# State space output projection: the last two value chunks, with their gate chunks, by seven products instead of eight

## The chip, the cores and the metric

The kernel runs on one core of one Trainium2 chip. The metric is the device time of one execution, in microseconds, as the median of the runs. A separate profiled execution gives the page and the trace.

## The reference

The program is a decoder trunk of two layers on 256 tokens of width 2048. Each layer has a token mixer, an attention to 256 memory tokens and a squared-ReLU MLP, each with an RMS norm before it and a residual add after it; a last norm closes the trunk. The token mixer of layer 0 is a chunked gMLP, that of layer 1 a state space layer with a gated output:

```python
_, states = lax.associative_scan(combine, (a, bu), axis=0)
y = jnp.einsum('gcp,sbgp->bsgc', cmat, states).real + d_skip.astype(F32) * u
y = jax.nn.gelu(y.reshape(bsz, seq, B_WIDTH), approximate=False).astype(h.dtype)
val, gate = jnp.split(y @ w_out + b_out, 2, axis=-1)
return val * jax.nn.sigmoid(gate)
```

All of it is float32. The change touches only the last two lines: `y` is 256 x 2048, `w_out` 2048 x 4096, its left half giving the values and its right half the gates.

## The kernel before

**Precision.** A float32 operand is split into a high half (rounded to the fast matmul format, by ScalarE, L103) and a low half (the rest, by VectorE, L104). A product of two operands takes three matmuls: high by high, low by high, high by low.

**Tiling.** Contraction runs over 16 k tiles of 128. Weights come in raw tiles of two k tiles by 512 columns (512 KB), loaded on the SP queue by `wload` (L127) into four raw buffers, split by `wtile` into three buffers each for high and low halves (`whi`, `wlo`). For one such slice `gemm_tok` (L159) runs 12 matmuls of 128 x 512: two k tiles, two token tiles t, three products. The activations are the stationary operand. After each slice `tick` advances a plan of small delayed tasks (`at(delay, task)`).

**The stage.** `s5` runs the scan, chunk by chunk, and then the output projection. The output has four value chunks of 512 columns (0 to 3) and four gate chunks (numbered 4 to 7 in the weights, `NCH + j`). For each j the kernel computes value chunk j and gate chunk `NCH + j`, adds the biases from PSUM (L1443, L1444; each bias is a row broadcast to 128 partitions by a load on POOL's queue, L113), takes the sigmoid of the gate on ScalarE (L1445), multiplies (L1446) and adds to the residual x (L1447), all of them 1024 wide. One tick later the next norm takes the chunk: squares summed on ScalarE (L198), 8 transposes on TensorE (L236), scaling into high and low halves on ScalarE and VectorE (L245, L246). Chunks 0 and 1 are interleaved by k, because the last features of the scan come late; chunks 2 and 3 are four plain calls of `gemm_tok`.

**Seven products.** `gemm_seven` multiplies a block of 2 token tiles x 2 column chunks x 2 slices (four k tiles) by 7 products in place of 8, as in Strassen's scheme in Winograd's form, and the other slices of both chunks directly. It needs four combinations of the activations (`sums`, from `token_sums`), four raw weight tiles at once, a buffer `run` for combined weights (L821, L827, L834, L841 on VectorE), and four 512-wide homes in which ScalarE keeps partial results copied from PSUM (`keep`, L812). Its matmuls are at L776. Between the products it places direct slices, and it ends with two direct slices taken in halves, so that each pair of PSUM banks is closed on its own. Before the change it serves the attention's values and output projection, and the second MLP's down projection (there with blocks of eight k tiles). It takes two adjacent column chunks, `n0` and `n0 + 1`.

**Order.** A framework schedules each engine's instructions ahead of time, by program order among those ready in its own estimate of time, and adds the semaphores. Each engine then runs its list in that order. Buffers of a pool with the same tag share slots, and a new tile waits for the old one's last reader.

**Buffers named by the change.** In `s5`, `resp` is four tiles of 128 x 1024 with the response matrices of the scan (`dq` in the profile); tags `qq`, `us`, `vv`, `u` and `pq` belong to scan tiles of 128 x 1024 each. The scan has finished with them when chunk 1 of the output begins.

Of the kernel before, what the change touches and what calls it, by code (L numbers as in the profile page):

```python
# [9 lines left out]
F32 = mybir.dt.float32  # L10
F32R = mybir.dt.float32r
I32 = mybir.dt.int32
AF = mybir.ActivationFunctionType
ALU = mybir.AluOpType
AX = mybir.AxisListType

P = 128
D = 2048
S = 256
KT = D // P  # L20
NB = 512
NCH = D // NB
KB = 2
# [15 lines left out]
class Trunk:  # L39
# [707 lines left out]
                    made.add(k)  # L747
        return raw, t1, t2, load, add

    def gemm_seven(self, tiles, token, sums, w, n0, k0, gather, end=None, own=None, ahead=None, then=None):  # L750

        nc = self.nc
        v = nc.vector
        kc0 = k0 // KB
        ws, run, kept = tiles
        raw, half = {}, lambda t: t.rearrange("p (k c) -> p k c", k=KB)  # L760

        def fetch(i, j):
            t = ws()
            self.fed = nc.sync.dma_start(out=half(t), in_=w[n0 + j, kc0 + i]).ins
            raw[i, j] = t

        def parts(src, own=None):
            hi, lo = (own() if own else self.wp.tile([P, KB * NB], F32R, name=nm) for nm in ("whi", "wlo"))
            self.split(hi, lo, src)
            return half(hi), half(lo)  # L770

        begun = set()

        def into(key, kts, left, hi, lo):
            out = banks[key]
            mm = lambda s, m, e: nc.tensor.matmul(out, s, m, start=key not in begun, stop=e, skip_group_check=True)  # L776
            for kk in kts:
                ah, al = left(kk)
                mm(ah, hi[:, kk, :], False)
                begun.add(key)  # L780
                mm(al, hi[:, kk, :], False)
            for kk in kts:
                mm(left(kk)[0], lo[:, kk, :], True)

        def block(key, t, i, src, more=None):
            into(key, range(KB), lambda kk: token(KB * i + kk, t), *parts(src))
            if ahead:
                into(key, range(KB), lambda kk: token(KB * (2 + i) + kk, t), *parts(more))

        def summed(key, k, src, more=None):  # L790
            into(key, range(KB), lambda kk: [f[:, k, kk, :] for f in sums[0]], *parts(src, own))
            if ahead:
                into(key, range(KB), lambda kk: [f[:, k, kk, :] for f in sums[1]], *parts(more))

        todo = {j: list(range(4 if ahead else 2, KT // KB)) for j in range(2)}

        def direct(j, first):

            kc = todo[j].pop(0)
            hi, lo = self.wtile(w, n0 + j, kc0 + kc)  # L800
            for t in (first, 1 - first):
                into((t, j), range(KB), lambda kk: token(KB * kc + kk, t), hi, lo)
                yield
            self.tick()

        def whole(*a):
            for _ in direct(*a):
                pass

        def keep(key, i):  # L810
            t = kept(i)
            nc.scalar.copy(out=t, in_=banks[key])  # L812
            return t

        acc = [self.psA.tile([P, 2, NB], F32, name="acc") for _ in range(2)]
        banks = {(1, 0): acc[0][:, 0], (0, 1): acc[0][:, 1], (0, 0): acc[1][:, 0], (1, 1): acc[1][:, 1]}
        for i, j in ((0, 0), (0, 1), (1, 0), (1, 1)):
            fetch(i, j)
        run = run()
        far, t1, t2 = ahead[:3] if ahead else ({}, None, None)  # L820
        v.tensor_tensor(out=run, in0=raw[0, 1], in1=raw[0, 0], op=ALU.subtract)  # L821
        summed((0, 1), 0, run, t1)
        block((1, 0), 0, 0, raw[0, 0], far.get((0, 0)))
        m5, m1 = keep((0, 1), 0), keep((1, 0), 1)
        block((0, 0), 0, 1, raw[1, 0], far.get((1, 0)))
        whole(1, 1)
        v.tensor_tensor(out=run, in0=raw[1, 1], in1=run, op=ALU.subtract)  # L827
        if ahead:
            ahead[-1](1)
        summed((1, 0), 1, run, t2)  # L830
        gather(0, n0, m1)
        u2 = keep((1, 0), 2)
        whole(1, 1)
        v.tensor_tensor(out=raw[0, 1], in0=raw[1, 1], in1=raw[0, 1], op=ALU.subtract)  # L834
        if ahead:
            ahead[-1](2)
        summed((1, 0), 2, raw[0, 1], far.get((0, 1)))
        gather(0, n0 + 1, u2)
        u3 = keep((1, 0), 3)
        whole(0, 0)  # L840
        v.tensor_tensor(out=run, in0=raw[1, 0], in1=run, op=ALU.subtract)  # L841
        if ahead:
            v.tensor_tensor(out=t1, in0=far[1, 0], in1=t2, op=ALU.subtract)
        block((1, 0), 1, 1, run, t1)
        whole(1, 1)
        summed((0, 1), 3, raw[1, 1], far.get((1, 1)))
        if then:
            then[-2]()
        v.tensor_tensor(out=u3, in0=u3, in1=m5, op=ALU.add)
        whole(0, 0)  # L850
        gather(1, n0 + 1, u3)
        while len(todo[0]) > 1 or len(todo[1]) > 1:
            j = len(todo[1]) > len(todo[0])
            whole(j, j)
        if then:
            then[-1](0)
        ends = [direct(0, 1), direct(1, 0)]
        for keys in (((1, 0), (0, 1)), ((0, 0), (1, 1))):
            for e in ends:
                next(e)  # L860
            for t, j in keys:
                (end or gather)(t, n0 + j, banks[t, j])
        for e in ends:
            next(e, None)
# [359 lines left out]
    def s5(self, x, cur, nxt):  # L1224
        nc, a, tc = self.nc, self.a, self.tc
        hT = cur.act
        NQ = G // NCH
        with tc.tile_pool(name="s5", bufs=2, reuse_waits="tile") as sp:
            yT = self.new_act()
            st = {}  # L1230

            ahead = {}
# [8 lines left out]
            resp = [sp.tile([P, T * P], F32, name=f"dq{i}", bufs=1) for i in range(4)]  # L1241
# [162 lines left out]
            for n in range(NCH):  # L1404
# [3 lines left out]
                chunks(n, acc)  # L1408
                follow(n)

            nxt.start()
            wo = a["b_w_out"]
            for j in range(NCH):
                if j == 0:
                    spare = self.psM.pop()
                    av1 = [spare.tile([P, NB], F32, name="ps") for _ in range(2)]
                    part = lambda n, acc, k: self.gemm_tok(yT, wo, n, acc=acc, kts=range(*k), first=k[0] == 0,
                                                           last=k[1] == KT)
                    av, _, ag = (part(n, acc, (0, 4)) for n, acc in ((0, None), (1, av1), (NCH, None)))
                    for k in (4, 8):  # L1420
                        for n, acc in ((0, av), (1, av1), (NCH, ag)):
                            part(n, acc, (k, k + 4))
                    self.flush()
                    for n, acc in ((0, av), (NCH, ag)):
                        part(n, acc, (12, KT))
                elif j == 1:
                    av = part(1, av1, (12, KT))
                    ag = self.gemm_tok(yT, wo, NCH + 1)
                else:
                    av = self.gemm_tok(yT, wo, j)  # L1430
                    ag = self.gemm_tok(yT, wo, NCH + j)
                cs = slice(j * NB, (j + 1) * NB)
                bv = self.bc(sp, a["b_b_out"][j * NB:(j + 1) * NB])
                bg = self.bc(sp, a["b_b_out"][D + j * NB:D + (j + 1) * NB])
                val = sp.tile([P, 2, NB], F32, name="val", tag="pq", bufs=4)
                gat = sp.tile([P, 2, NB], F32, name="gat", tag="pq", bufs=4)
                b2 = lambda b: b.unsqueeze(1).broadcast_to([P, 2, NB])
                if j == 1:
                    for t in range(2):
                        nc.vector.tensor_tensor(out=val[:, t], in0=av1[t], in1=bv, op=ALU.add)  # L1440
                    self.psM.append(spare)
                else:
                    nc.vector.tensor_tensor(out=val, in0=av, in1=b2(bv), op=ALU.add)  # L1443
                nc.vector.tensor_tensor(out=gat, in0=ag, in1=b2(bg), op=ALU.add)  # L1444
                nc.scalar.activation(out=gat, in_=gat, func=AF.Sigmoid)  # L1445
                nc.vector.tensor_tensor(out=val, in0=val, in1=gat, op=ALU.mult)  # L1446
                nc.vector.tensor_tensor(out=x[:, :, cs], in0=x[:, :, cs], in1=val, op=ALU.add)  # L1447
                self.at(1, lambda j=j: nxt.chunk(x, j))
# [185 lines left out]
```

## Time and profile before

| what | value |
|---|---|
| median of 3 runs | 2772.53 us (2771.16 to 2774.17) |
| profiled execution | 2768.95 us |
| its span, first to last instruction | 2767.2 us |
| granted TensorE clock in it | 0.999 |
| TensorE matmuls | 14978, busy 2747.1 us |
| VectorE | busy 2046.0 us |
| ScalarE | busy 1421.1 us |
| weights of the stage (`b_w_out`) | 64 loads of 512 KB, issued from 1474.6 to 1673.3 us |

The span is what the trace covers; the profiled execution's own time is 1.75 us longer, and differs from the median of the other runs by 3.6 us. In the rows, times are microseconds from the span's start unless marked ns; PE is TensorE's matmuls and PEld its weight loads, DVE is VectorE, ACT ScalarE, POOL GpSimd and SP the queue that issues most loads. A row of the timeline gives the start, the length, the engine, the line, what is written from what, and in brackets the idle time before it with what ended it. Overlapping matmuls make each row longer than the step from one to the next.

### The profile page before, as it was taken

The numbers are of one execution on the slowest core, as the hardware profiler recorded it, in microseconds if no ns is written. First come the engines' busy times: TensorE is split into PE (matmuls) and PEld (weight loads), VectorE is DVE, ScalarE is ACT, GpSimd is POOL, SyncE is SP. The second block draws the span as 40 slices with busy tenths as digits, with TensorE's granted clock in tenths as the row PEclk, the third lists the DMA queues.
The fourth block names the chain that finished last, engine by engine and source line by source line (L and its number), as shares of the span: only waits on it lengthen the run. The fifth ranks groups of instructions, "written<-read, shape, count | busy, mean of one in ns | idle before, by whom it ended". The sixth has DMA issues, their size and how long they took to land. (4 is left out here: it accounts for less than half of the span.)

```text
span 2767.2 us, 39486 instructions
## 1 busy us (share of the span) xinstructions
PE 2747.1 (99%) x14978; PEld 2326.5 (84%) x14978; DVE 2046.0 (74%) x2809; ACT 1421.1 (51%) x1814; POOL 186.7 (7%) x331
## 2 busy tenths in 40 slices
PE   9999999999999999999999999999999999999998
PEld 7888888888888888888888888888888888888887
DVE  6865756778888878787577667557767978869685
ACT  6545544555544434444566445445555655546454
POOL 0100000001011111111203100000000000000000
PEclk9999999999999999999999999999999999999999
DMA  8766665557788888886879767565557557475565
GB/s 298 231 196 230 202 183 181 170 159 231 220 281 258 262 258 256 266 256 221 235 238 288 214 202 231 182 195 153 182 163 232 176 174 244 153 248 163 177 212 159
DMA packets 194175, 593.75 MB, mean 215 GB/s; under 512 B 44096, under 2 KB 45168, under 8 KB 193472
## 3 DMA queue, kind: packets, MB, share of 16 engines
q1 hardware_dynamic: 153456, 537.46, 61.3%
q0 software_dynamic: 40000, 52.71, 6.8%
q8 instruction: 117, 1.92, 0.3%
q10 hardware_dynamic: 528, 1.06, 0.1%
q14 instruction: 74, 0.61, 0.1%
HBM read 567.51 MB, written 23.46 MB: 214 GB/s over the span
## 5 line engine op out<-in xcount | busy, mean ns | idle before, releaser
L104 DVE TENSOR_TENSOR wlo<-wraw,whi 128x1024 fp32r<-128x1024 f32 (+1 forms) x865 | 1051.3, 1221 | 444.5 <-ACT whi L103 438.2
L103 ACT CAST whi<-wraw 128x1024 fp32r<-128x1024 f32 (+1 forms) x865 | 909.2, 1053 | 812.2 <-PE acc L875 181.2
L174 PE MATMUL acc<-act,whi 128*128 128x512 f32 x3072 | 740.9, 391 | 0.6 <-DVE act L246 0.6
L174 PEld LDWEIGHTS acc<-act,whi 128*128 128x128 f32 x3072 | 563.1, 188 | 110.7 <-issue 1.4
L179 PEld LDWEIGHTS acc<-act,wlo 128*128 128x128 f32 x3072 | 395.0, 191 | 17.0 <-DVE wlo L104 1.4
L179 PE MATMUL acc<-act,wlo 128*128 128x256 f32 x3072 | 403.2, 283 | 1.2 <-DVE wlo L104 0.8
L159 PE MATMUL acc<-whi,act 128*128 128x512 f32 x1472 | 369.4, 393 | 5.4 <-ACT whi L103 5.4
L159 PEld LDWEIGHTS acc<-whi,act 128*128 128x128 f32 x1472 | 274.8, 189 | 62.6 <-ACT whi L103 5.6
L776 PE MATMUL acc<-whi,act 128*128 128x512 f32 x864 | 233.0, 392 | 0.1
L875 PE MATMUL acc<-whi,hl 128*128 128x512 f32 x544 | 212.7, 391 | 0.0
L874 PE MATMUL acc<-whi,hh 128*128 128x512 f32 x544 | 212.6, 391 | 0.0
L159 PE MATMUL acc<-wlo,act 128*128 128x512 f32 x736 | 197.2, 389 | 0.0
L776 PEld LDWEIGHTS acc<-whi,act 128*128 128x128 f32 x864 | 160.3, 188 | 36.8 <-ACT ends L812 1.9
L159 PEld LDWEIGHTS acc<-wlo,act 128*128 128x128 f32 x736 | 138.3, 188 | 28.9
L877 PE MATMUL acc<-wlo,hh 128*128 128x512 f32 x544 | 145.8, 389 | 0.0
L776 PE MATMUL acc<-wlo,act 128*128 128x512 f32 x432 | 133.1, 390 | 0.0
L190 ACT COPY r<-acc 128x512 f32<-128x512 f32 x64 | 37.7, 589 | 162.9 <-PE acc L174 162.8
L875 PEld LDWEIGHTS acc<-whi,hl 128*128 128x128 f32 x544 | 102.1, 188 | 22.2 <-issue 1.0
L776 PE MATMUL acc<-whi,hh 128*128 128x512 f32 x308 | 120.5, 391 | 0.0
L874 PEld LDWEIGHTS acc<-whi,hh 128*128 128x128 f32 x544 | 102.1, 188 | 21.4 <-issue 0.2
L877 PEld LDWEIGHTS acc<-wlo,hh 128*128 128x128 f32 x544 | 102.0, 188 | 21.4 <-issue 0.2
L776 PE MATMUL acc<-whi,hl 128*128 128x512 f32 x308 | 119.9, 389 | 0.0
(373 smaller groups left out, 2883.5 us busy)
## 6 DMA issues: line engine op xcount, KB each, us to landing
wraw<-in_f_w_up SPq DMA_DIRECT2D x256, 512.0 KB, 4.4
wraw<-in_f_w_down SPq DMA_DIRECT2D x200, 512.0 KB, 5.0
wraw<-in_x_w_q SPq DMA_DIRECT2D x64, 512.0 KB, 4.3
wraw<-in_x_w_k SPq DMA_DIRECT2D x64, 512.0 KB, 4.4
wraw<-in_b_w_out SPq DMA_DIRECT2D x64, 512.0 KB, 4.5
wraw<-in_a_w_in SPq DMA_DIRECT2D x63, 512.0 KB, 4.5
wraw<-in_x_w_v SPq DMA_DIRECT2D x48, 512.0 KB, 4.4
wraw<-in_x_w_o SPq DMA_DIRECT2D x48, 512.0 KB, 4.4
```

Of the source, the lines that this page charges most:

```text
L103: self.nc.scalar.copy(out=hi, in_=src)
L104: return self.nc.vector.tensor_tensor(out=lo, in0=src, in1=hi.bitcast(F32), op=ALU.subtract).ins
L159: nc.tensor.matmul(out[t], a[:, kt, sl], b[:, kk, :], start=st and a is ah, stop=en)
L174: nc.tensor.matmul(acc[:, f, :], hi[:, kk, sl], both[:, kt].rearrange("p a s -> p (a s)"), start=first and kk == 0, stop=last and kk == FK ...
L179: nc.tensor.matmul(acc[:, f, 0:S], lo[:, kk, sl], ah[:, kt, :], start=False, stop=last and kk == FK - 1, skip_group_check=True)
L190: nc.scalar.copy(out=dst, in_=acc[:, :, S:])
L776: mm = lambda s, m, e: nc.tensor.matmul(out, s, m, start=key not in begun, stop=e, skip_group_check=True)
L874: nc.tensor.matmul(acc[:, t, :], ah, hi[:, kk, :], start=kt == 0, stop=False)
L875: nc.tensor.matmul(acc[:, t, :], al, hi[:, kk, :], start=False, stop=False)
L877: nc.tensor.matmul(acc[:, t, :], hid[kt // 4][0][:, kt % 4, sl], lo[:, kk, :], start=False, stop=kt == KT - 1)
```

## The change

Value chunk j and gate chunk `NCH + j`, for j = 2 and 3, go through `gemm_seven` as a pair. It gets a parameter `step`, the distance between the pair's columns in chunks (`NCH`, 4). The first four k tiles of each pair take the seven products, the other 12 go directly.

Three ticks into chunk 1, `block_sums` rebuilds the first four k tiles of the activations from their two halves and forms the four combinations, once for both pairs. The four raw tiles of a pair are loaded into `resp`; `run`, the kept partial results and the sums take the slots of other scan tiles.

The bias loads stand at the head of each pair. Kept partial results get the bias as they are gathered (`part`). At the close of each bank (`end`), VectorE adds the kept result (or, where there is none, the bias) to PSUM, 512 wide; for a gate ScalarE takes the sigmoid; when value and gate of a token tile are both done, VectorE multiplies them and adds to x. The next norm's task for chunk j still runs one tick after the pair.

```diff
-    def gemm_seven(self, tiles, token, sums, w, n0, k0, gather, end=None, own=None, ahead=None, then=None):
+    def gemm_seven(self, tiles, token, sums, w, n0, k0, gather, end=None, own=None, step=1, ahead=None, then=None):
...
-            self.fed = nc.sync.dma_start(out=half(t), in_=w[n0 + j, kc0 + i]).ins
+            self.fed = nc.sync.dma_start(out=half(t), in_=w[n0 + step * j, kc0 + i]).ins
...
-            hi, lo = self.wtile(w, n0 + j, kc0 + kc)
+            hi, lo = self.wtile(w, n0 + step * j, kc0 + kc)
...
+            def block_sums():
+                y = sp.tile([P, 4, S], F32, name="ysum", tag="qq", bufs=4)
+                nc.vector.tensor_tensor(out=y, in0=yT[0][:, 0:4].bitcast(F32), in1=yT[1][:, 0:4].bitcast(F32), op=ALU.add)
+                sums.append(self.token_sums(sp.tile([P, KB * NB], F32, name="s", tag="qq", bufs=4),
+                                            lambda: sp.tile([P, 4, 2, P], F32R, name="sums", tag="us"),
+                                            y[:, 0:2], y[:, 2:4]))
+
+            def gated_pair(j):
+                cs = slice(j * NB, (j + 1) * NB)
+                bias = [self.bc(sp, a["b_b_out"][o + j * NB:o + (j + 1) * NB]) for o in (0, D)]
+                val = sp.tile([P, 2, NB], F32, name="val", tag="pq", bufs=4)
+                gat = sp.tile([P, 2, NB], F32, name="gat", tag="pq", bufs=4)
+                held, done = {}, set()
+                v = nc.vector
+
+                def part(t, n, p):
+                    v.tensor_tensor(out=p, in0=p, in1=bias[n - j], op=ALU.add)
+                    held[t, n - j] = p
+
+                def end(t, n, src):
+                    out = (val, gat)[n - j][:, t]
+                    v.tensor_tensor(out=out, in0=src, in1=held.get((t, n - j), bias[n - j]), op=ALU.add)
+                    if n > j:
+                        nc.scalar.activation(out=out, in_=out, func=AF.Sigmoid)
+                    done.add((t, n - j))
+                    if (t, 0) in done and (t, 1) in done:
+                        v.tensor_tensor(out=val[:, t], in0=val[:, t], in1=gat[:, t], op=ALU.mult)
+                        v.tensor_tensor(out=x[:, t, cs], in0=x[:, t, cs], in1=val[:, t], op=ALU.add)
+
+                run = sp.tile([P, KB * NB], F32, name="run", tag="u", bufs=1)
+                keep = [sp.tile([P, 2, NB], F32, name="keep", tag="vv") for _ in range(2)]
+                homes = iter(resp)
+                self.gemm_seven((lambda: next(homes), lambda: run, lambda i: keep[i // 2][:, i % 2]),
+                                lambda kt, t: [f[:, kt, t * P:(t + 1) * P] for f in yT[:2]],
+                                sums, wo, j, 0, part, end, step=NCH)
...
             for j in range(NCH):
+                if j == 1:
+                    self.at(3, block_sums)
+                if j >= 2:
+                    gated_pair(j)
+                    self.at(1, lambda j=j: nxt.chunk(x, j))
+                    continue
...
-                else:
-                    av = self.gemm_tok(yT, wo, j)
-                    ag = self.gemm_tok(yT, wo, NCH + j)
```

More of the change, by code (lines that the diff above doesn't have):

```diff
@@ L1411, in s5 @@
             nxt.start()
             wo = a["b_w_out"]
+            sums = []
             for j in range(NCH):
+                if j == 1:
[4 more added lines that the diff above has]
+                    continue
                 if j == 0:
@@ L1425, in s5 @@
                         part(n, acc, (12, KT))
-                elif j == 1:
+                else:
                     av = part(1, av1, (12, KT))
                     ag = self.gemm_tok(yT, wo, NCH + 1)
-                else:
-                    av = self.gemm_tok(yT, wo, j)
-                    ag = self.gemm_tok(yT, wo, NCH + j)
                 cs = slice(j * NB, (j + 1) * NB)
```

## The prediction

> **What bounds the kernel now.** I read the page first, for the busiest engine and the chain that ended last.
>
> ```profile
> span 2767.2 us, 39486 instructions
> PE 2747.1 (99%) x14978; PEld 2326.5 (84%) x14978; DVE 2046.0 (74%) x2809; ACT 1421.1 (51%) x1814; POOL 186.7 (7%) x331
> ...
> PE 37%; DVE 1%; ACT 0%; DMA 0%; issue 0%; DVEq 0%; ACTq 0%
> ```
>
> TensorE is busy for 99% of the span and is nearly all of the chain. A busy PE row can still hide gaps, so next comes the timeline of the stage itself: one slice of weights (two k tiles, twelve matmuls: eight with the high half, four with the low half), and the end of the stage, where L174 begins.
>
> ```profile
> 1643.48 1.98 PE L159 MATMUL acc<-whi,act 128*128 128x512 f32 x8
> 1643.86 1.22 DVE L104 TENSOR_TENSOR wlo<-wraw,whi 128x1024 fp32r<-128x1024 f32 x1 [1.49 <-ACT whi L103]
> 1645.49 1.06 ACT L103 CAST whi<-wraw 128x1024 fp32r<-128x1024 f32 x1 [1.66 <-PE acc L159]
> 1646.20 1.98 PE L159 MATMUL acc<-whi,act 128*128 128x512 f32 x8
> ...
> 1690.67 1.98 PE L174 MATMUL acc<-act,whi 128*128 128x512 f32 x8
> ```
>
> From 1643.48 to 1646.20 is 2.72 us for twelve matmuls, 0.2267 us each. In each slice VectorE idles 1.49 us and ScalarE 1.66 us, waiting for work that TensorE frees. The stage is bound by TensorE alone, so fewer matmuls are worth their own time. Chunk 3 with its gate runs from 1646.20 to 1690.67, 44.47 us: sixteen slices are 43.52, and the eight transposes of the chunk before take the other 0.95.
>
> **The products saved.** One pair has 16 slices of 12 matmuls, 192. In sevens, the first four k tiles take 7 products of 6 instead of 8: 186. Two pairs save 12 matmuls, 12 x 0.2267 = **-2.72 us**. The Trainium skill, "TensorE: Matmul & The Clock Gate", section "Wait — 56ns, not 53.3ns?", gives 512 columns ÷ 2.4 GHz + 2.5 ns, 215.7 ns; by that estimate the term would be -2.59. The row here shows 227 ns, and the row decides.
>
> **What the seven-product form costs elsewhere.** The memory attention already runs this routine, so its output projection (its second pair) is the nearest row.
>
> ```profile
> 2023.81 0.88 PEld L776 LDWEIGHTS acc<-whi,sums 128*128 128x128 f32 x4
> ...
> 2068.15 1.77 PEld L174 LDWEIGHTS acc<-act,whi 128*128 128x128 f32 x8
> ```
>
> ```profile
> PEld acc L776 <- ACT ends L812: 0.9, 4, 0.3
> PEld acc L776 <- ACT kept L812: 0.7, 3, 0.3
> ```
>
> That pair is 186 matmuls and 16 transposes in 44.34 us. Less 2 x 0.95 for transposes and 186 x 0.2267 = 42.16, there remain 0.28 us. The second fence (waits of weight loads, 1860 to 2080 us, four such calls) names its cause: a bank must be copied out by ScalarE (L812) before the next product overwrites it; 1.6 us over four calls, 0.4 per call at the load, of which 0.28 reached the matmuls. For two pairs I take **+0.56**; bounds 0 and 0.8.
>
> Added work on VectorE and ScalarE, priced from the same operations elsewhere:
>
> ```profile
> L821 DVE TENSOR_TENSOR run<-ws x15: 1212/1221/1227, 465.3 to 2656.0; 128x1024 f32<-128x1024 f32 x15
> L722 DVE TENSOR_TENSOR ws<-r x8: 414/416/418, 2087.2 to 2621.8; 128x256 f32<-128x256 f32 x8
> L104 DVE TENSOR_TENSOR sums<-ws,sums x8: 1218/1219/1220, 2101.1 to 2636.0; 128x1024 fp32r<-128x1024 f32 x8
> L103 ACT CAST sums<-ws x8: 1046/1047/1051, 2099.8 to 2634.7; 128x1024 fp32r<-128x1024 f32 x8
> L849 DVE TENSOR_TENSOR ends<-ends x8: 682/684/685, 490.8 to 2041.2; 128x512 f32<-128x512 f32 x8
> L812 ACT COPY ends<-acc x16: 565/577/591, 477.6 to 2039.2; 128x512 f32<-128x512 f32 x16
> ```
>
> The block sums, once, during chunk 1: one 1024-wide add (1.22), four of 0.416, one low half (1.22): 4.1 us of VectorE and 1.05 of ScalarE. They are first read by pair 2, more than six slices later, and each slice leaves 1.49 us, so three slices absorb them; I cost them at 0. Without that cover it is 4.1.
>
> Each pair adds three splits (3 x 1.22 VectorE, 3 x 1.05 ScalarE), four weight subtractions (4.88), three part additions and one sum of parts (4 x 0.68 = 2.73), and four copies (2.3 ScalarE). Over a whole pair VectorE rises from 25.7 to about 37 of 44 us, which fits. It is uneven though: the seven products and five slices between them take 102 matmuls, 23.1 us and 0.95 for transposes, and in them VectorE has 12 splits (14.65), 4.88, 2.73, the ends of the chunk before, and 1.75 for that chunk's scaling. For the second pair the ends are six 512-wide operations (4.1): **28.1 us of VectorE in 24.1 us of TensorE**. For the first it is the old closing of chunk 1, three of 1.22: 27.7. So it lives on splits made ahead. How the attention's own pair gets through the same stretch:
>
> ```profile
> 1646.20:1669.40 23.20, 23.20 (x108) 19.18 (x107) 15.07 (x16) 12.66 (x18) 0.54 (x1) 1.00 0.67 198
> 2023.81:2046.39 22.58, 22.58 (x108) 18.46 (x106) 20.74 (x27) 18.39 (x32) 0.00 (x0) 1.00 0.33 98
> ```
>
> (window, sum, then PE, PEld, DVE, ACT, POOL busy.) VectorE is busy 20.74 of 22.58 us there against 15.07 of 23.20 in the present stage, and only the 0.28 was lost. Its tight place is the start:
>
> ```profile
> 2024.64 1.28 DVE L636 TENSOR_TENSOR x<-acc,x 128x512 f32<-128x512 f32 x2
> 2025.84 1.22 DVE L104 TENSOR_TENSOR wlo<-ws,whi 128x1024 fp32r<-128x1024 f32 x1
> 2026.97 1.22 DVE L104 TENSOR_TENSOR wlo<-wraw,whi 128x1024 fp32r<-128x1024 f32 x1
> 2027.67 0.62 PE L776 MATMUL acc<-wlo,act 128*128 128x512 f32 x2
> ```
>
> The low half of the third product is ready at 2027.06 and used at 2027.67: 0.61 us to spare. In the changed kernel the two 512-wide additions there (1.28) are followed by multiply and add for t = 0, and after the sigmoid for t = 1: 2 x 1.38 more. The split after it is ready at 2028.19 and due 1.36 after 2027.67, 0.84 to spare. If all the added operations stand ahead of the two splits, that second one is 2.75 - 0.84 = 1.9 us late. The attention's values close with an equal load (seven operations, ScalarE between them):
>
> ```profile
> 1978.24 1.22 DVE L104 TENSOR_TENSOR wlo<-ws,whi 128x1024 fp32r<-128x1024 f32 x1
> 1978.50 1.13 PE L776 MATMUL acc<-whi,act 128*128 128x512 f32 x4
> 1979.70 0.63 PE L776 MATMUL acc<-wlo,act 128*128 128x512 f32 x2
> 1980.17 2.01 PE L776 MATMUL acc<-whi,act 128*128 128x512 f32 x8
> ```
>
> There the program sets eight high matmuls of the next slice in a row and other work between; from 1978.50 to 1980.17 are 1.67 us for a product of 1.36 and two short matmuls of another stage, so at most 0.3 is lost. That is the nearer row: I take **+0.4** for pair 2 to pair 3, bounds 0 and 1.9.
>
> Into pair 2, chunk 1's closing is spaced as now:
>
> ```profile
> 1601.66 1.98 PE L159 MATMUL acc<-whi,act 128*128 128x512 f32 x8
> 1605.36 1.22 DVE L104 TENSOR_TENSOR wlo<-wraw,whi 128x1024 fp32r<-128x1024 f32 x1
> 1607.63 1.22 DVE L104 TENSOR_TENSOR wlo<-wraw,whi 128x1024 fp32r<-128x1024 f32 x1
> ```
>
> With products of 1.36 us the low halves made at 4.92 and 7.19 us after the start (1606.58, 1608.85) would be due at about 5.0 and 7.7. They fit by 0.1 and 0.5; one subtraction (1.22) among them loses 1.1. I take **+0.1**, bounds 0 and 1.1.
>
> **DMA.** The bytes are the same; four of sixteen slices go to the state buffers, idle by then, which lets them be loaded earlier. The bias loads move to the head of a pair:
>
> ```profile
> L113 POOL DMA_DIRECT2D bc<-in_b_b_out x6: 538/538/585, 1569.8 to 1647.9; - x6
> DMA to landing us min/median/max: 4.0/4.1/7.3
> ```
>
> The value bias of pair 3 needs the buffer that pair 2's first ends release, about 1.3 us before pair 3 starts. It lands 4.1 later, 2.8 us into the pair, and is first added no sooner than twelve matmuls and a copy, 3.3 us in. If it is late, VectorE waits with the splits behind it, and TensorE for those; the slowest landing, 7.3, would come 6 us in, and the splits ahead cover part of the 2.7 lacking. I cost it at 0, bounds 0 and 1. POOL has nothing queued behind it until the attention's loads.
>
> **The end of the stage.**
>
> ```profile
> 1690.87 1.23 DVE L1444 TENSOR_TENSOR gat<-acc,bc 128x1024 f32<-128x1024 f32 x1 [1.31 <-PE acc L159]
> 1695.50 1.22 DVE L1447 TENSOR_TENSOR x<-x,val 128x1024 f32<-128x1024 f32 x1
> 1696.77 0.85 PEld L236 LDWEIGHTS ps<-ident,x 128*128 128x128 f32 x8 [0.35 <-DVE x L1447]
> ```
>
> Closing chunk 3 now takes 1690.87 to 1696.72. In halves, half of it runs before the last matmuls end, the rest is four short operations, about 3 us. At most the 0.35 wait of the transposes goes; **-0.1**, bounds -0.35 and 0.3.
>
> **Sum.** -2.72 + 0.56 + 0.4 + 0.1 - 0.1 = -1.76. The profiled execution took 2768.95 us, so it would become 2767.2. The median of the runs is 2772.53, 3.6 above it; the same step gives **2770.8**.
>
> **Rivals.** *All cost hidden* (as the attention's values hide theirs): -2.72 - 0.35 = -3.1, 2769.5. For it speaks that TensorE waits almost nowhere in these calls; against it the L812 waits, present in each.
>
> *VectorE becomes the bound.* In the sevens stretches its excess is 28.1 - 24.1 = 4.0 and 27.7 - 24.1 = 3.6 us. If the splits ahead cover none of it, 7.6 - 2.72 = +4.9, 2777.4: slower. It decides from the point where the excess beyond the splits ahead passes 2.7 us. For it: the 20.74 of 22.58. Against it: that stretch has as many operations (two chunks scaled instead of one, fewer in the ends) and lost 0.28. The Trainium skill, same page, section "Architectural detail", says that VectorE and ScalarE are strict FIFO: a multiply waiting for its sigmoid would hold the splits behind it, as this rival needs; the 1.31 idle of L1444 does not show what stood behind it.
>
> *A load waits in the wrong place.* If the last raw tile of pair 3 stands in the load queue ahead of pair 2's later slices, it waits for the seventh product's split, about 20 us in, and the slices behind it land 4.5 later, split by 25.4 where 22.6 is due: 2.8 us, -1.76 + 2.8 = +1.0, 2773.6. Against it: the attention's raw tiles are loaded by the same call, and no such wait shows.
>
> **How the numbers follow.** Forecast 0.62, all hidden 0.18, VectorE 0.12, load 0.08. Best of the bounds -3.1, worst of the pairs' and the end's +0.8 + 1.9 + 1.1 + 0.3 - 2.72 = +1.4; the runs of before spread from 1.4 below their median to 1.6 above. So the range is 2772.5 - 3.1 - 1.4 = 2768.0 to 2772.5 + 1.4 + 1.6 = 2775.5, to which the bias adds half a microsecond: 2776.0. Most of the VectorE case stays outside. About 0.2%, 5.5 us, is what a measurement of this kernel can tell from no change. No case gains so much: faster 0.04, for what I miss. Slower needs the VectorE case and a little more: 0.08. The rest, 0.88, is no change.
>
> **What would show it.** 14966 matmuls, L776 with 372 more and L159 with 384 fewer; the two pairs' windows at about 43.4 and 43.8 us against 44.47; weight loads waiting for L812 under 1 us; VectorE nearly full for 20 us at each pair's start. Wrong: TensorE waiting for L104 or L103 by more than 2 us in a pair, a load or bias wait named there, or a gain over 3.1, which would have to come from outside the stage.

## The result, and the profile after

The changed kernel takes **2775.06 us** (median of 22 runs, 2771.67 to 2780.46). The kernel before, measured again beside it, takes 2771.36 us (22 runs, 2766.98 to 2775.90). The ratio is 1.0013, 95% interval 1.0007 to 1.0019: **slower by 0.13%**, where a small gain was forecast. The profiled execution took 2774.34 us, 5.39 more than the one before. The page of the kernel after:

```profile
span 2772.6 us, 39524 instructions
...
PE 2748.4 (99%) x14966; PEld 2325.7 (84%) x14966; DVE 2069.2 (75%) x2845; ACT 1429.1 (52%) x1831; POOL 185.1 (7%) x331
...
PE acc L776 26%; PE acc L174 24%; PE acc L159 14%; PE acc L179 13%; PE acc L875 4%; PE acc L874 4%; PE acc L877 4%; DMA dq<-Kd 1%; PE ps L532 1%; PE ps L610 1%; DVE wlo L104 1%; PE ps L236 0%; DMA memc<-in_mem_t 0%; PE ps L159 0%; PE ps L1180 0%
```

The twelve matmuls are gone (14978 to 14966), yet TensorE is busy 1.3 us longer: some matmuls ran slower. The last line, the chain by line, names a transfer that the change never mentions, `dq<-Kd`: the scan's last response tiles. TensorE's own waits from 1552 to 1760 us, first in the kernel before, then after:

```profile
PE ps L1349 <- DMA dq<-Kd: 1.1, 1, 1.1
```

```profile
PE ps L1349 <- DMA dq<-Kd: 4.8, 1, 4.8
PE acc L174 <- ACT whi L103: 0.9, 2, 0.6
```

(waited for, then us in total, times, longest.) No matmul wait is named inside the two pairs. The new ones stand before them, at L1349, and after them, at L174. So I cut the timeline at five starts. At the scan's end, L1349 multiplies by the response tiles, L1357 by the Q tiles, L1372 transposes the last features. Timeline before, then after:

```profile
1545.97 1.21 PE L1357 MATMUL ps<-qq,vv 64*32 64x128 f32 x64
1552.80 0.65 PE L1349 MATMUL ps<-dq,us 128*32 128x128 f32 x16
1554.51 0.64 PE L1349 MATMUL ps<-dq,us 128*32 128x128 f32 x16 [1.06 <-DMA dq<-Kd]
1555.08 1.21 PE L1357 MATMUL ps<-qq,vv 64*32 64x128 f32 x64
1559.08 1.04 PE L1372 MATMUL ps<-ident,y 128*128 128x128 f32 x8
...
1736.79 0.28 PE L532 MATMUL ps<-kh,qh 128*128 128x256 f32 x1
```

```profile
1545.63 1.21 PE L1357 MATMUL ps<-qq,vv 64*32 64x128 f32 x64
1552.44 0.64 PE L1349 MATMUL ps<-dq,us 128*32 128x128 f32 x16
1557.88 1.08 PE L1349 MATMUL ps<-dq,us 128*32 128x128 f32 x16 [4.79 <-DMA dq<-Kd]
1558.89 1.96 PE L1357 MATMUL ps<-qq,vv 64*32 64x128 f32 x64
1564.47 1.04 PE L1372 MATMUL ps<-ident,y 128*128 128x128 f32 x8
...
1607.06 1.10 PE L776 MATMUL acc<-whi,sums 128*128 128x512 f32 x4
1650.41 0.87 PE L776 MATMUL acc<-whi,sums 128*128 128x512 f32 x3
1694.31 1.98 PE L174 MATMUL acc<-act,whi 128*128 128x512 f32 x8
1741.98 0.28 PE L532 MATMUL ps<-kh,qh 128*128 128x256 f32 x1
```

The last response tile is waited for 4.79 us instead of 1.06, and behind that wait the same rows take longer: the 16 of L1349 1.08 instead of 0.64, the 64 of L1357 1.96 instead of 1.21. From the first L1357 to L1372 are 13.11 us before and 18.84 after. The two pairs take 1650.41 - 1607.06 = 43.35 and 1694.31 - 1650.41 = 43.90, where they took 44.54 and 44.47. From the first L174 to the first L532, the stretch of the attention's first projection, are 46.12 us before (from 1690.67) and 47.67 after.

| stretch | before | after | difference |
|---|---|---|---|
| scan's end (L1357 to L1372) | 13.11 | 18.84 | +5.73 |
| from there to pair 2 | 42.58 | 42.59 | 0 |
| pair 2 | 44.54 | 43.35 | -1.19 |
| pair 3 | 44.47 | 43.90 | -0.57 |
| attention's first projection | 46.12 | 47.67 | +1.55 |
| all else | | | -0.1 |

The sum is the 5.4 us between the spans. The pairs gained 1.76 us; the loss lies outside them.

**The scan's end.** What happens there is seen on SP's queue after, and in the windows of 6 us, before and then after (length, busy PE, PEld, DVE, ACT, POOL, granted clock, share of the transfer engines, GB/s):

```profile
1545.77 0.91 SPq L764 DMA_DIRECT2D dq<-in_b_w_out  x1
1550.28 0.33 SPq L127 DMA_DIRECT2D wraw<-in_b_w_out  x1
1550.84 0.33 SPq L764 DMA_DIRECT2D dq<-in_b_w_out  x1
```

```profile
1540.00:1546.00 6.00, 6.00 (x60) 4.67 (x58) 2.26 (x2) 1.06 (x1) 0.56 (x1) 1.00 1.06 279
1546.00:1552.00 6.00, 6.00 (x89) 4.99 (x86) 1.97 (x2) 2.10 (x2) 0.00 (x0) 1.00 0.88 272
```

```profile
1546.00:1552.00 6.00, 6.00 (x79) 4.95 (x64) 2.53 (x3) 1.05 (x1) 0.00 (x0) 1.00 0.97 323
1552.00:1558.00 6.00, 1.21 (x23) 0.61 (x25) 2.58 (x5) 2.94 (x3) 0.00 (x0) 0.82 0.64 218
1558.00:1564.00 6.00, 6.00 (x90) 4.63 (x90) 3.50 (x3) 1.28 (x3) 0.00 (x0) 0.61 0.66 247
```

L764 is the raw load of a pair in sevens. The framework lets it go as soon as its home, a response tile, is read for the last time: at 1545.77 us, 61 us before pair 2, while POOL's last response load (issued at 1543.44) is on its way. From 1546 to 1552 us the engines are 0.97 busy instead of 0.88; from 1552 on the clock is 0.82 and then 0.61.

But POOL's last response loads went out later too. Their issue, and the time that the very last of them took from issue to landing, before and then after:

```profile
1537.62 2.94 POOL L1239 DMA_DIRECT2D dq<-Kd  x5 [4.84 <-DMA dq<-Kd]
DMA to landing us min/median/max: 14.4/14.4/14.4
```

```profile
1540.21 0.59 POOL L1239 DMA_DIRECT2D dq<-Kd  x1 [5.20 <-DMA dq<-Kd]
1543.44 0.58 POOL L1239 DMA_DIRECT2D dq<-Kd  x1 [2.64 <-DMA dq<-Kd]
DMA to landing us min/median/max: 14.3/14.3/14.3
```

The last response load goes out at 1540.0 us before and at 1543.44 after, since POOL stood for earlier response loads to land, and it takes 14.4 and 14.3 us. So in these two profiles the longer wait comes from the later issue, 2.3 us ahead of the first raw load, which cannot have caused it. What the raw loads add has to be read from runs and from more profiles.

**The attention.** Its first two memory tiles lie where the last chunk's value and gate tiles were, in both kernels. POOL's load of them and ScalarE's first use, before and then after:

```profile
1697.26 1.06 POOL L300 DMA_DIRECT2D memc<-in_mem_t  x2 [48.80 <-issue]
1702.54 2.24 ACT L254 ACTIVATE act<-memc,gcol 128x256 fp32r<-128x256 f32 x5 [1.35 <-DMA memc<-in_mem_t]
```

```profile
1700.20 0.69 DVE L1439 TENSOR_TENSOR x<-x,val 128x512 f32<-128x512 f32 x1
1701.43 1.06 POOL L300 DMA_DIRECT2D memc<-in_mem_t  x2 [51.72 <-ACT whi L103]
1707.68 1.71 ACT L254 ACTIVATE act<-memc,gcol 128x256 fp32r<-128x256 f32 x4 [3.06 <-DMA memc<-in_mem_t]
1712.52 2.11 PE L174 MATMUL acc<-act,whi 128*128 128x512 f32 x8 [0.27 <-ACT whi L103]
```

The load goes out 0.5 us after the last addition to x: 6.59 us after the first L174 before, 7.12 after. ScalarE stands for it 3.06 us instead of 1.35, with the weight splits of the projection behind it in its list, and TensorE waits for two of these.

### The profile page after: what moved, and what is told of

It is laid out like the page before. It is cut to its first block, busy times and chain, and to the rows that moved or that the text cites. A ratio compares the mean times of both kernels' runs of the same rounds, so it can differ in the third digit from the quotient of the medians.

```text
span 2772.6 us, 39524 instructions
## 1 busy us (share of the span) xinstructions
PE 2748.4 (99%) x14966; PEld 2325.7 (84%) x14966; DVE 2069.2 (75%) x2845; ACT 1429.1 (52%) x1831; POOL 185.1 (7%) x331
## 3 DMA queue, kind: packets, MB, share of 16 engines
q10 hardware_dynamic: 528, 1.06, 0.1%
## 4 chain that ended last, share of the span: by engine, by line
PE 96%; DMA 2%; DVE 1%; ACT 1%; issue 0%; POOL 0%; DVEq 0%; ACTq 0%
PE acc L776 26%; PE acc L174 24%; PE acc L159 14%; PE acc L179 13%; PE acc L875 4%; PE acc L874 4%; PE acc L877 4%; DMA dq<-Kd 1%; PE ps L532 1%; PE ps L610 1%; DVE wlo L104 1%; PE ps L236 0%; DMA memc<-in_mem_t 0%; PE ps L159 0%; PE ps L1180 0%
## 5 line engine op out<-in xcount | busy, mean ns | idle before, releaser
L103 ACT CAST whi<-wraw 128x1024 fp32r<-128x1024 f32 (+1 forms) x857 | 899.3, 1051 | 790.9 <-PE acc L875 176.4
L174 PE MATMUL acc<-act,whi 128*128 128x512 f32 x3072 | 741.9, 391 | 1.5 <-ACT whi L103 0.9
L174 PEld LDWEIGHTS acc<-act,whi 128*128 128x128 f32 x3072 | 562.9, 188 | 112.1 <-ACT whi L103 1.8
L179 PEld LDWEIGHTS acc<-act,wlo 128*128 128x128 f32 x3072 | 395.0, 191 | 17.4 <-DVE wlo L104 1.5
L159 PEld LDWEIGHTS acc<-whi,act 128*128 128x128 f32 x1216 | 227.6, 189 | 53.0 <-ACT whi L103 5.4
L776 PEld LDWEIGHTS acc<-whi,act 128*128 128x128 f32 x1080 | 200.7, 188 | 45.8 <-ACT ends L812 1.9
L159 PEld LDWEIGHTS acc<-wlo,act 128*128 128x128 f32 x608 | 114.4, 188 | 23.8
```

Of the source, the lines that this page charges most:

```text
L103: self.nc.scalar.copy(out=hi, in_=src)
L159: nc.tensor.matmul(out[t], a[:, kt, sl], b[:, kk, :], start=st and a is ah, stop=en)
L174: nc.tensor.matmul(acc[:, f, :], hi[:, kk, sl], both[:, kt].rearrange("p a s -> p (a s)"), start=first and kk == 0, stop=last and kk == FK ...
L179: nc.tensor.matmul(acc[:, f, 0:S], lo[:, kk, sl], ah[:, kt, :], start=False, stop=last and kk == FK - 1, skip_group_check=True)
```

## The experiments

Three theories stood. *Early loads*: the raw loads share the transfer engines with the scan's last tiles; the wait and the clock behind it cost about 4 us. *Chance*: the wait at the scan's end varies by itself and the loss is elsewhere. *Late memory tile*: the value and gate tiles of the last pair hold up the attention. Each ratio below is against the kernel before on the same chip. It is not the quotient of the two medians beside it, so where the two differ both are given.

### 1. Raw loads behind the direct loads

```diff
-            self.fed = nc.sync.dma_start(out=half(t), in_=w[n0 + step * j, kc0 + i]).ins
+            with self.tc.issue_after(self.fed) if step > 1 else nullcontext():
+                self.fed = nc.sync.dma_start(out=half(t), in_=w[n0 + step * j, kc0 + i]).ins
```

> The changed kernel with one edit: the raw loads of the two pairs may be issued only after the direct weight load that stands before them in the program, so on SP's queue the four of pair 2 stand behind sixteen direct loads instead of among the first eight, and no longer beside the last response tiles of the scan. Theory of the early loads (the raw tiles share the transfer engines with the scan's last response tiles, TensorE waits for these 4.79 us instead of 1.06, and then multiplies at a lower clock for some 2 us): the wait of the scan's second-half outputs for a response tile falls back to 2 us or less, the pairs stay at about 43.4 and 43.9 us, and the time is 3 to 5.5 us below the changed kernel, which is at the kernel before or up to 2 us under it. Theory of chance (that wait differs from execution to execution whatever is loaded beside it, and the loss lies elsewhere): the wait may be anything, and the time stays within 1.5 us of the changed kernel.

2770.96 us against 2770.69, ratio 0.9994 (0.9986 to 1.0003); for the changed kernel it was 1.0013, so this edit is worth some 0.19%, 5 us; by the medians (3.70 us above the kernel before, then 0.27) it is 3.4 us. Scan's end:

```profile
1554.33 0.64 PE L1349 MATMUL ps<-dq,us 128*32 128x128 f32 x16 [1.36 <-DMA dq<-Kd]
1554.91 1.21 PE L1357 MATMUL ps<-qq,vv 64*32 64x128 f32 x64
1558.93 1.04 PE L1372 MATMUL ps<-ident,y 128*128 128x128 f32 x8
```

The wait is 1.36 us and the rows behind it are at full speed. The order of the loads is the only thing moved and the intervals of the two ratios do not meet, so the early issue is part of the cause. The short wait of this one profile proves less: POOL's last response load happened to go out early here, at 1539.7 us. The pairs took 43.38 and 44.25. Yet the kernel isn't faster than the one before: the attention's stretch is 48.62 us here, and eats the pairs' gain.

### 2. The early loads alone, in the kernel before

```diff
                 else:
+                    for i, t in enumerate(resp if j == 2 else ()):
+                        nc.sync.dma_start(out=t.rearrange("p (k c) -> p k c", k=KB), in_=wo[j + i % 2 * NCH, i // 2])
                     av = self.gemm_tok(yT, wo, j)
```

> The kernel before with one addition: the four raw tiles of pair 2 are loaded into the idle response tiles at the places of SP's queue where the changed kernel has them (after four direct loads, then one by one), and nothing reads them; no multiplication is saved. It moves 2 MB more than the kernel before. Theory of the early loads: the scan's end loses 3 to 5 us to the wait and the clock, nothing else changes, and the time is 3 to 5 us above the kernel before. Theory of chance: within 1 us of the kernel before.

2776.00 us against 2770.69, ratio 1.0016 (1.0007 to 1.0025): the early loads by themselves make the kernel before slower, by 4 to 5 us. They are 2 MB on top of what it moves; experiment 1, where the bytes are equal, agrees. But its profile was of its fastest run (2769.90 us) and shows a wait of only 1.88. So it was profiled twice more, and the kernel before once more:

> The kernel before with the four early raw loads once more, for a profile of a common execution: the first profile was of the fastest of its twelve runs (2769.9 us, median 2776.0). If the early loads cost their time at the scan's end, a profile near the median shows a wait of 3 to 6 us for the last response tiles ahead of the scan's second-half outputs and the multiplications behind it stretched by a lower clock, and everything from the output projection on as long as before.

> The same kernel a third time: time above the first profile's and wait ahead of the scan's second-half outputs should rise together, by 1 us of wait for 1 us of time and some 2 us more once the clock drops.

> The kernel before once more: if its spread from 2768 to 2777 us is the same wait at the scan's end, its wait there and its time differ from the first profile's (1.06 us, 2768.95 us) by the same amount; if not, the time differs elsewhere.

They took 2777.49, 2772.30 and 2771.33 us. The first of these, timeline and windows:

```profile
1555.15 0.72 PE L1349 MATMUL ps<-dq,us 128*32 128x128 f32 x16 [0.52 <-DMA dq<-Kd]
1561.19 1.08 PE L1349 MATMUL ps<-dq,us 128*32 128x128 f32 x16 [5.31 <-DMA dq<-Kd]
```

```profile
1552.00:1558.00 6.00, 3.36 (x28) 2.27 (x26) 2.45 (x2) 1.16 (x2) 0.00 (x0) 0.98 0.99 331
1558.00:1564.00 6.00, 2.81 (x80) 2.16 (x80) 0.00 (x0) 0.00 (x0) 0.00 (x0) 0.50 0.69 233
```

That is the changed kernel's picture without any product in sevens: 5.83 us of waiting, then the clock at 0.50. Its scan's end is 19.38 us, the second profile's 14.32 (a wait of 2.25 us, clock 1.00), the kernel before's 12.88 (a wait of 0.83). Against that last one the stretch is 6.5 and 1.4 us longer, the time 6.2 and 1.0. So time follows this stretch. The kernel before's own two profiles, though, do not: 13.11 and 12.88 us here, 2768.95 and 2771.33 in all; 1.39 of those 2.4 us lie in the attention's stretch (46.12 and 47.51).

### 3. The same waits with a sixteenth of the bytes

```diff
-                        nc.sync.dma_start(out=t.rearrange("p (k c) -> p k c", k=KB), in_=wo[j + i % 2 * NCH, i // 2])
+                        nc.sync.dma_start(out=t[:, 0:64], in_=wo[j + i % 2 * NCH, i // 2][:, 0, 0:64])
```

> As the kernel before with the four early loads into the response tiles, but each brings 64 of the 1024 elements of a row: 32 KB in place of 512 KB, at nearly the same places of SP's queue and with the same waits for the response tiles; nothing reads them. Theory that the bytes matter (they share the transfer engines with the scan's last response tiles): the cost of the early loads goes, the time is within 1.2 us of the kernel before. Rival, that the waits matter (SP stands in order behind a load that waits for a response tile to come free, and the direct loads behind it come late): the time stays 3 to 6 us above the kernel before, as with full loads.

2772.33 us against 2771.86, ratio 1.0004 (0.9995 to 1.0013). SP still stood for the response tiles:

```profile
1546.99 1.58 SPq L1431 DMA_DIRECT2D dq<-in_b_w_out  x2
1552.29 1.62 SPq L127 DMA_DIRECT2D wraw<-in_b_w_out  x2
```

The scan's end took 12.90 us with a wait of 0.83. With the waits kept and the bytes gone the cost is 0.47 us by the medians, where full loads cost 5.31: it is the bytes, though the intervals of the two ratios overlap between 1.0007 and 1.0013. (The small loads stand in twos on the queue, not one by one; that is the one other difference.)

### 4. The last pair's value and gate tiles elsewhere

```diff
-                val = sp.tile([P, 2, NB], F32, name="val", tag="pq", bufs=4)
-                gat = sp.tile([P, 2, NB], F32, name="gat", tag="pq", bufs=4)
+                val = sp.tile([P, 2, NB], F32, name="val", tag="qq" if j == 3 else "pq", bufs=4)
+                gat = sp.tile([P, 2, NB], F32, name="gat", tag="qq" if j == 3 else "pq", bufs=4)
```

> The changed kernel with one edit: the value and gate tiles of the last pair lie in two idle slots of the Q tiles, so that the attention's first two memory tiles, whose place they held, can be loaded before the pair's last addition to x. The order of the instructions on every engine stays as it was. Theory that the late memory tile is what makes ScalarE, and behind it TensorE, wait in the attention's first projection: the two waits of TensorE for a weight split there (0.27 and 0.64 us) go, the stretch from the first matmul of the query projection to the end of its 46 to 48 us comes down by about 1.5 us, and the time is 1 to 2 us below the changed kernel. Rival, that the stretch differs because of VectorE's work at the close of the last pair and not because of the memory tile: the time stays within 0.7 us of the changed kernel.

2773.26 us against 2770.69, ratio 1.0005 (0.9997 to 1.0014). POOL's loads, and TensorE's waits from 1552 to 1760 us:

```profile
1650.65 0.53 POOL L300 DMA_DIRECT2D memc<-in_mem_t  x1
1658.22 0.53 POOL L300 DMA_DIRECT2D memc<-in_mem_t  x1 [7.04 <-DVE x L1439]
```

```profile
PE ps L1349 <- DMA dq<-Kd: 5.0, 2, 3.3
```

From the first L174 (1695.26 here), the first two memory tiles are loaded 52 and 45 us earlier than in the changed kernel, and no wait for a split is left: the stretch is 45.56 us, 2.1 below the changed kernel's. The scan's end, untouched, is 18.73 us. The gain is 0.08%, 2.2 us, by the ratios and 1.1 by the medians, about the expected size, but the intervals overlap; the stretch is what shows it.

### 5. Both edits

> Both edits together: raw loads behind the direct loads, and the value and gate tiles of the last pair in idle slots. If the early loads cost 3 to 5.5 us and the late memory tile 1 to 2, and the two are separate, the time is 4 to 7 us below the changed kernel, 0.5 to 3 us below the kernel before: what is left then is the 1.76 us that the pairs gained and what the attention no longer waits. If the loss at the scan's end was chance, at most 2 us below the changed kernel.

2768.35 us against 2770.69, ratio 0.9986 (0.9977 to 0.9994): **faster than both kernels**. Its profile has the attention's stretch at 45.58, the pairs at 43.38 and 43.91, and a scan's end of 16.05. So a late tile comes without early loads too, if less: POOL issued its last response load at 1543.42, as late as in the changed kernel, TensorE waited for it 2.48 us, and the clock fell behind it. Windows of 1 us:

```profile
1557.00:1558.00 1.00, 1.00 (x37) 0.62 (x23) 1.00 (x2) 0.31 (x2) 0.00 (x0) 0.50 0.00 0
...
1560.00:1561.00 1.00, 1.00 (x5) 0.78 (x5) 0.00 (x0) 0.00 (x0) 0.00 (x0) 0.86 0.89 287
```

### 6. What of that is the pairs'

The memory tile could be moved in the kernel before as well, so the edit of experiment 4 was made there, with both edits in the changed kernel run again beside it, and the changed kernel profiled once more.

> The kernel before with the one edit that the attention's memory tiles gained from: the value and gate tiles of the last chunk in two idle slots of the Q tiles; every engine's order as before, all chunks plain. If the late memory tile costs the kernel before as well (its stretch from the query projection's first matmul to the end of it took 46.12, 46.57, 46.81, 47.01, 47.26 and 47.51 us in the profiles with plain chunks, and 45.56 and 45.58 us with the tiles elsewhere), the stretch is about 45.6 us and the time 0.6 to 2 us below the kernel before. If only the pairs in seven products close so late that it matters, no change within 0.6 us.

> Raw loads behind the direct loads and the tiles elsewhere, once more, beside the kernel before with the same tiles elsewhere: the pairs alone should tell the two apart, by 1.76 us as the profiles have it, so that this one is 1 to 2.5 us below that and 2 to 4 us below the kernel before. If the gain of this kernel was all from the memory tile, the two are equal within 0.6 us.

> The changed kernel once more, for a second profile: if its first was a common one, the wait ahead of the scan's second-half outputs is again 3 to 6 us with a lowered clock behind it, the pairs take 43.4 and 43.9 us, and the query projection's stretch lies between 47 and 49 us. If that wait was chance, it is 1 to 2.5 us and the time below 2772 us.

The kernel before with the tiles elsewhere: 2770.24 us against 2771.28, ratio 0.9997 (0.9988 to 1.0006). Its stretch is 45.61 us, as expected, but the time can't tell that from no change. Both edits in the changed kernel: 2767.69 us, ratio 0.9988 (0.9979 to 0.9996), 2.55 us below the former where the pairs account for 1.76; but the two intervals overlap, so the pairs' gain rests on their steps in the profiles. The changed kernel again: 2775.91 us, a wait of 5.97 us at the scan's end, pairs of 43.41 and 43.94 us, a stretch of 49.41 in the attention. Its first profile was a common one.

All thirteen profiles, by stretch in us, with the last response load: how long before the first L1357 it was issued, and how long it took to land:

| raw loads, tiles | scan's end | attention's stretch | issued before | took |
|---|---|---|---|---|
| plain chunks, no early loads (2 profiles) | 13.11, 12.88 | 46.12, 47.51 | 6.0, 6.4 | 14.4, 14.5 |
| plain, small early loads | 12.90 | 47.01 | 5.9 | 14.0 |
| plain, tiles elsewhere | 11.86 | 45.61 | 7.0 | 13.6 |
| plain, early loads (3) | 13.96, 19.38, 14.32 | 46.57, 46.81, 47.26 | 6.1, 4.0, 6.0 | 15.3, 17.3, 15.6 |
| sevens, early loads (2: the change) | 18.84, 19.99 | 47.67, 49.41 | 2.2, 4.1 | 14.3, 17.4 |
| sevens, early loads, tiles elsewhere | 18.73 | 45.56 | 3.1 | 15.6 |
| sevens, late loads | 13.43 | 48.62 | 5.8 | 14.5 |
| sevens, late loads, tiles elsewhere (2) | 16.05, 12.71 | 45.58, 45.59 | 2.4, 6.3 | 12.2, 14.3 |

The scan's end has a mean of 17.5 us in the six profiles with early full loads and 13.3 in the other seven: +4.3. The attention's stretch has a mean of 48.6 in the three with sevens and the tiles in place, 46.9 in the six with plain chunks and the tiles in place: +1.7. With the pairs' -1.76 that makes +4.2, where the medians say +3.7.

The last two columns part the +4.3. With early loads the last response load took 15.9 us to land on average, without them 13.9: 2.0 longer. It also went out 1.4 us later on average, and the raw loads of the same execution cannot have done that: in all six profiles the first of them is issued within 0.3 us of the first L1357, which is 2.3 us or more after the last response load. Where POOL was in time (5.8 to 7.0 us before), early loads lengthen the scan's end by some 1.3 us, from a mean of 12.8 to 14.1; where it was late (2.2 to 4.1), by some 3, from 16.05 (one profile) to a mean of 19.2.

## Why the prediction was wrong

**Right: the pairs.** The steps inside them came to -2.72 + 0.56 + 0.4 + 0.1 = -1.66; the two profiles of the changed kernel give -1.76 and -1.66 against 44.54 and 44.47, the four others with sevens -1.38 to -1.76. The sum fits; its terms were not measured one by one. The matmul counts fell as said. VectorE was to be nearly full for 20 us at each pair's start, and was, to 9.97 and 9.96 of 10 us in the second 10 us of each. Windows, then waits of weight loads in the two pairs, both after:

```profile
1617.00:1627.00 10.00, 10.00 (x45) 8.04 (x44) 9.97 (x12) 6.31 (x10) 0.54 (x1) 1.00 0.79 249
1660.41:1670.41 10.00, 9.88 (x43) 7.69 (x42) 9.96 (x13) 5.65 (x8) 0.00 (x0) 1.00 0.35 107
```

```profile
PEld acc L776 <- DVE wlo L104: 0.8, 2, 0.5
PEld acc L776 <- ACT keep L812: 0.5, 2, 0.3
```

TensorE lacked 0.12 us of 10 there, so the rival of VectorE as the bound fell, and the L812 waits stayed under 1 us. "All cost hidden" fell too: about 1 us of cost did show in the pairs.

**Wrong: the step on DMA**, which decided the sign. It said that the raw tiles go to buffers that are idle "which lets them be loaded earlier", and priced that at nothing, as if earlier were harmless. It named the moment from which the tiles are idle and never looked at what the transfer engines do at that moment. The view for it, windows with the DMA share, would have shown 0.88 to 1.06 of the engines in use from 1540 to 1552 us in the kernel before, and the 1.06 us that TensorE already waited for the scan's last tile. In place of 0 the step was worth 3.4 to 5.3 us, by the medians of three pairs of kernels that differ in the early loads: 5.3 in the kernel before (experiment 2), 3.4 in the changed kernel (experiment 1), 4.9 with the tiles elsewhere (experiment 4 against 5). Experiment 3 says that it needs the bytes. What the profiles show of the way is that the scan's last response tile lands later, TensorE waits for it, and the clock falls. Only part of that is explained: the longer landing, 2.0 us on average. In the first two profiles the scan's end was 5.7 us longer, 3.7 of waiting and 2.0 that the slower clock took, and there the 3.7 came from POOL's later issue. That these two pointed at the raw loads was partly luck.

The raw loads slow the response loads: with full early loads the last response load took 14.3 to 17.4 us from issue to landing, in the seven other profiles 12.2 to 14.5. The Trainium skill, "DMA: Bandwidth & Descriptors", section "Queues, rings and completion order", says that each transfer engine takes turns between the queues that have work, packet by packet. The trace agrees as far as that slowing goes. How the turns are shared no run here shows.

**Wrong in size: the end of the stage.** Its step counted the closing of chunk 3 as a gain of 0.1, "about 3 us" after the last matmuls. The last addition to x ended 6.58 us after the first L174, against 6.05 before, since VectorE's list has three weight splits among the short operations. The price lies not there but in who waits for these tiles: the attention's memory tiles, which the step doesn't name. It was +1.7 us in place of -0.1 (means above); with the tiles elsewhere the stretch is 45.56 to 45.61 in four profiles, so with the place free nothing of that difference is left. Why 0.53 us of later issue becomes 1.7 us stays open: the loads landed later too, and a wait in ScalarE's list moves all the splits behind it.

**The rivals.** "A load waits in the wrong place" had the right kind of cause, a load queue, but looked for it inside the pairs, where no wait is. No rival asked what the early loads collide with. The time did fall in the range, but by luck: its upper end came from VectorE and the spread of runs, neither of which was the cause.

**Open.** Without early loads the scan's end still varied from 11.86 to 16.05 us. POOL issued the last response load late in four of the six profiles with early loads and in one of the seven others. That may be chance in so few, or the early loads may favour it; no run here tells, though the runs' 3.4 to 5.3 us are more than the 1.3 to 3 at a like issue. In all thirteen profiles a response load goes out no sooner than 0.28 us after the landing of the one eight places ahead of it: the last one after, issued at 1543.44 us, follows a landing at 1543.15. So a slow landing is handed on to a later issue. Whether the framework or the chip sets this limit, and what made the earlier landing slow, wasn't tried.

## What to carry to other kernels

A buffer that comes free early is an invitation to a scheduler: a load into it goes out at once, and "earlier" has to be priced like any other edit, by the DMA share of the window in which it will now run and by what else lands there. Here one ordering line that holds the loads back was worth more than the products saved. And when a tile's last use moves, look up which later tile takes its place: that load is the one that waits.

## What the runs showed of the hardware

TensorE's clock fell after waits that I'd have thought too short to matter. After 2.25 us of idling it stayed at 1.00; after 2.48 in another profile it fell to 0.50 for 3.41 us; after 4.79, 5.31 and 5.97, and after 1.73 and 3.30 with 16 matmuls between them, for 6.83. 3.41 us at half the clock cost a busy TensorE some 1.7 us on top of the wait, by estimate from these two numbers. In all thirteen traces the clock changes only at whole steps of 3.41 us from its first rise, and it matters how a gap falls on the steps: the gap of 2.48 us put 2.29 us of idling into one of them, that of 2.25 us was cut into 1.07 and 1.18.

The Trainium skill, "TensorE: Matmul & The Clock Gate", section "What's actually happening", speaks of a window of about 3.4 us, free-running, that has to be idle before the gate closes, and as long a busy one to open it. The steps and the recovery agree with it. That the window has to be idle throughout does not: the clock fell after steps with 1.75 (at 1524.91 in the kernel before with tiles elsewhere), 1.94, 2.29, 2.36 and 2.73 us of idling, unless the thinly filled matmuls around count as partly idle, which no run here shows. Idling alone doesn't decide it either, for a step with 1.90 us of it (1478.75 to 1482.17 in the profile with small loads) left the clock at 1.00.
